# Expert weights split in larger pieces, and result additions issued one phase later

## The chip, the cores and the metric

The kernel runs on one core of one Trainium2 chip. The metric is device microseconds of one execution. Before the change it is 1491.45 us, the median of 3 runs (1490.14 to 1492.38). The profiled execution took 1492.99 us, of which 1490.9 us lie between its first and last instruction, at a mean granted TensorE clock of 0.988 of full speed.

## The reference, cut to what matters

Two decoder layers on 256 tokens of 1024 features. The second layer ends in a mixture of eight experts, and that part is all that the change touches:

```python
def swiglu(x, w_gate, w_up, w_down):
    return (jax.nn.silu(x @ w_gate) * (x @ w_up)) @ w_down

def moe_ffn(x, router_w, w_gate, w_up, w_down):      # top 2 of 8 experts for each token
    ...
    def expert_block(args):
        tok_b, e_b = args
        xb = xf[tok_b]                                # the expert's tokens
        return swiglu(xb, w_gate[e_b], w_up[e_b], w_down[e_b])
    ...                                               # w_gate, w_up: 8 x 1024 x 3584, w_down: 8 x 3584 x 1024
    y = y * w_buf[:, None]                            # times the gate
    out = jax.ops.segment_sum(y, tok_buf, num_segments=T)
```

All arrays are float32. The expert weights are 352 MB, read once.

## The kernel before, in words

**Splitting.** TensorE multiplies float32r. To keep float32 accuracy a weight piece `raw` is split in two: `wh`, the rounded copy, made by ScalarE (ACT, line 177), and `wl = raw - wh`, made by VectorE (DVE, line 180). The activations are split in the same way. TensorE (PE) then sums products: for a stationary block of activations it takes `wh` with the high and the low part and `wl` with the high part only.

**Pieces.** A piece is one load: 1 x 1792 columns of `w_gate` or `w_up` (896 KB), or 2 x 1024 of `w_down` (1 MB), into one of seven 8 KB buffers per partition ("ring"). `halves` splits it in two halves of 896 or 1024 columns, one instruction each on ACT and on DVE; the halves take turns between two pools, each with four pairs of 4 KB buffers (`wpool`, `wpool2`). A load into a ring buffer waits until DVE has split what was in it.

**Phases.** An expert's 3584 hidden features are done in two chunks of 1792 (`c` = 0, 1). Each chunk is a gate phase (8 pieces, PSUM banks "mm" and "gd"), then Silu into `hh` (line 1194), an up phase (8 pieces, the same bank names), the product into `hh` (line 1217), and later, woven into the next chunk's phases, its 7 down pieces, which add up in two banks "b". Four experts after the first are done in full width (128 tokens, "wide"), three in 64 tokens ("narrow": experts 2, 4 and 6 in order of time). A narrow expert stacks high and low activations in one stationary block, so each half needs 4 products for a wide one's 6. The last of its 8 pieces is not split; it is multiplied as float32, and the low rows are moved up through `room` (line 1121, ACT) and a product with `shift`. Silu, `room` and the multiplication into `hh` are pinned to their place in the order of their engine.

**Side work.** Lists of small steps (`side`) are popped one per piece: `to_features` (PE transposes `hh`, ACT and DVE make `hT`, lines 1137 to 1140), `combine` (two steps: ACT and DVE copy a result bank "b" into the one buffer `ys`, PE multiplies it with `DT` into a bank "a", DVE adds it to `x_in`, lines 1092 to 1099), `transposed` (makes `DT`), and `dispatch` (8 steps: PE gathers the next two experts' tokens with `D` into a bank "a", ACT copies them to `xg`, line 1023). In a second chunk the gate phase has 4 (narrow: 2) steps of `to_features`, 2 of `combine` and 1 of `transposed`; the up phase has the 8 of `dispatch`, when a group of experts is due. Bank "a" has two buffers. Each engine runs its instructions in one order, which a scheduler has fixed when the program was built, from the program's order and its own estimates; it can pull a step ahead of where the program has it.

Of the kernel before, what the change touches and what calls it, by code (L numbers as in the profile page):

```python
# [17 lines left out]
P = 128  # L18
T = 256
NB = 2  # L20
# [45 lines left out]
def trunk(ctx, tc, x, positions, w_in, conv_w, a_log, dt_bias, gdn_norm_w, lam_q1, lam_k1, lam_q2, lam_k2,  # L66
# [95 lines left out]
    def halves(ld, cut=1, count=2):  # L162

        raw, nk, cols = ld
        m = nk * cols // count
        for i in range(count):
            pool, size = wpool, WH
            if extra:
                turn[0] += 1
                if turn[0] % 2 == 0:  # L170
                    pool, size = extra[1], 1024
            wh = pool.tile([P, size], F32R, tag="wh", name=nm("wh"))
            wl = pool.tile([P, size], F32R, tag="wl", name=nm("wl"))
            n = m // (cut if i else 1)
            for c in range(0, m, n):
                w = raw[:, i * m + c:i * m + c + n]
                high = S.activation(wh[:, c:c + n], w, AF.Copy)  # L177
                if fence_high[0] is not None:
                    order(high, fence_high[0])
                low = V.tensor_tensor(wl[:, c:c + n], w, wh[:, c:c + n].bitcast(F32), op=ALU.subtract)  # L180
                if fence[0] is not None:
                    order(low, fence[0])
            yield i * (nk // count), wh, wl

    def piece(src, nk, cols, parts=1, cut=1):
        return halves(load(src, nk, cols, parts, cut), cut)
# [793 lines left out]
    def experts(xs, jobs, mp, ring2, rest, first):  # L980
# [22 lines left out]
        def dispatch(group, early=False):  # L1003
# [3 lines left out]
            Dt = mp.tile([P, NB, W], F32R, tag="ys", name=nm("D"))  # L1007
# [25 lines left out]
        def transposed(n):  # L1033
            Dt = mp.tile([P, NB, P], F32R, tag="ys", name=nm("D"))
# [16 lines left out]
        def products(outs, xg, narrow, k, parts, x32=None):  # L1051
# [5 lines left out]
            for i, (_, wh, wl) in enumerate(parts):  # L1057
                o = outs[2 * i:2 * i + 2]
                if not narrow:
                    xstat(o, [xg[:, 0:4], xg[:, 4:8]], k, 1, 0, wh, wl, CHUNK // 2, KD)  # L1060
                    continue
                x_ = xg[:, k].rearrange("p c s -> p (c s)")
                for w in (wh, wl):
                    for j in range(2):
                        mm(o[j], x_, w[:, j * BANK:(j + 1) * BANK], k == 0 and w is wh, False)

        def down_pieces(n, c, first=0, parts=1, cut=1):

            wd = weights(n, 2)[c * CHUNK:(c + 1) * CHUNK].rearrange("(p j) d -> p j d", j=NF)
            for f in range(first, NF, 2):  # L1070
                yield [(f + j, wh, wl) for j, wh, wl in piece(wd[:, f:f + 2, :], 2, D, parts, cut if f == NF - 2 else 1)]

        def down(subs, n, c, hT, py):
            for f, wh, wl in subs:
                K, k = NC * NF, c * NF + f
                if jobs[n][3]:
                    x_ = hT[:, f].rearrange("p c s -> p (c s)")
                    for w in (wh, wl):
                        for i, o in enumerate(py):
                            mm(o, x_, w[:, i * 512:(i + 1) * 512], k == 0 and w is wh, k == K - 1 and w is wl)  # L1080
                else:
                    for w in (wh, wl):
                        for c_ in range(2 if w is wh else 1):
                            for i, o in enumerate(py):
                                mm(o, hT[:, f, c_], w[:, i * 512:(i + 1) * 512], k == 0 and w is wh and c_ == 0,
                                   k == K - 1 and w is wl)

        def combine(n, py, DT):
            def part(i):
                ys = mp.tile([P, 2, 512], F32R, tag="ys", name=nm("ys"))  # L1090
                yh, yl = ys[:, 0], ys[:, 1]
                S.activation(yh, py[i], AF.Copy)  # L1092
                V.tensor_tensor(yl, py[i], yh.bitcast(F32), op=ALU.subtract)
                for b in range(NB):
                    pt = bank("a")
                    mm(pt, DT[:, b], yh, True, False)
                    mm(pt, DT[:, b], yl, False, True)
# [3 lines left out]
            return [lambda i=i: part(i) for i in range(2)]  # L1101
# [47 lines left out]
        side = []  # L1149
        tiles, steps = dispatch([jobs[n] for n in groups[0]], True)  # L1150
# [6 lines left out]
        for n, job in enumerate(jobs):  # L1157
# [5 lines left out]
            for c in range(NC):  # L1163
# [263 lines left out]
    with tc.tile_pool(name="ring2", bufs=1, reuse_waits="tile") as ring2, \  # L1427
            tc.tile_pool(name="wpool2", bufs=4, reuse_waits="tile") as wpool2, \
# [30 lines left out]
```

## Time and profile before

| | us |
|---|---|
| median of 3 runs | 1491.45 |
| profiled execution | 1492.99 |
| its span | 1490.9 |
| experts (from the first expert weights at work to the end) | some 540 to 1491 |
| PE busy | 1448.6 |
| DVE busy | 1218.3 |
| ACT busy | 1036.6 |

An engine's row says how long at least one of its instructions ran. For PE this includes the drain of pipelined matmuls, so it is not a measure of peak. The experts repeat: one wide and one narrow expert together take some 231 us, and the pattern returns with the next pair.

### The profile page before, as it was taken

To read this page: it belongs to the slowest core of one execution; us is meant where nothing else is said; L and a number is where in the kernel's file an instruction comes from. 1 tells how busy PE (TensorE), PEld (TensorE's weight loads), DVE (VectorE), ACT (ScalarE), POOL (GpSimd) and SP (SyncE) were. 2 spreads that over 40 slices of the span, in tenths; PEclk is the share of its full clock that TensorE was granted. 3 is DMA by queue.
4 is the path that set the end of the run, shared out by engine and by line. 5 is a ranking of instruction groups with operands and counts; after the bars stand their busy time and mean duration, and the time that the engine had idled before them with its cause. 6 is when DMAs were issued, how large, how long until landed. Compare 5 with 4: busy or idle time off the path is not lost.

```text
span 1490.9 us, 24038 instructions
## 1 busy us (share of the span) xinstructions
PE 1448.6 (97%) x8873; PEld 1233.1 (83%) x8873; DVE 1218.3 (82%) x1609; ACT 1036.6 (70%) x1553; POOL 23.7 (2%) x37
## 2 busy tenths in 40 slices
PE   8999999999999999999999999999999999999995
PEld 8978899998987889886698877588877589888884
DVE  6877655556796798989899989899989899989886
ACT  5748544456666587787797887886887877778763
POOL 1100000000000000000000000000000000000000
PEclk9999999999999999999999999999999999999998
DMA  9633455535533179999999999999999899999891
GB/s 322 219 106 118 153 195 195 193 121 196 193 113 100 54 298 363 386 371 374 380 394 384 375 390 394 356 393 408 352 379 417 335 395 413 338 357 395 292 394 34
DMA packets 89124, 433.93 MB, mean 291 GB/s; under 512 B 7816, under 2 KB 9992, under 8 KB 74912
## 3 DMA queue, kind: packets, MB, share of 16 engines
q1 hardware_dynamic: 87808, 428.54, 76.1%
q0 software_dynamic: 1184, 3.71, 0.9%
q8 instruction: 73, 1.20, 0.3%
q14 instruction: 59, 0.48, 0.1%
HBM read 431.17 MB, written 1.05 MB: 290 GB/s over the span
## 4 chain that ended last, share of the span: by engine, by line
PE 87%; DVE 7%; issue 2%; ACT 2%; DMA 0%; DVEq 0%; SPq 0%; ACTq 0%
PE ps_b L99 26%; PE ps_mm L99 25%; PE ps_gd L99 24%; PE ps_a L99 9%; DVE wl L180 4%; PE ps_a L1137 2%; ACT wh L177 1%; DVE x_in L1099 1%; PE ps_mm L566 0%; ACT junk L415 0%; DVE hT L1140 0%; ACT xT L240 0%; PE ps_gd L408 0%; PE ps_mm L670 0%; DVE D L999 0%
## 5 line engine op out<-in xcount | busy, mean ns | idle before, releaser
L180 DVE TENSOR_TENSOR wl<-raw,wh 128x896 fp32r<-128x896 f32 (+2 forms) x851 | 925.7, 1144 | 145.8 <-ACT wh L177 139.4
L177 ACT ACTIVATE wh<-raw 128x896 fp32r<-128x896 f32 (+2 forms) x851 | 792.4, 995 | 153.4 <-PE ps_gd L99 68.4
L99 PE MATMUL ps_b<-wh,hT 128*128 128x512 f32 x816 | 232.6, 396 | 0.7 <-ACT hT L1139 0.7
L99 PE MATMUL ps_gd<-wh,xg 128*128 128x448 f32 x808 | 218.8, 368 | 0.0
L99 PE MATMUL ps_mm<-wh,xg 128*128 128x448 f32 x808 | 212.5, 372 | 0.3
L99 PEld LDWEIGHTS ps_b<-wh,hT 128*128 128x128 f32 x816 | 152.0, 188 | 39.2 <-issue 6.4
L99 PEld LDWEIGHTS ps_gd<-wh,xg 128*128 128x128 f32 x808 | 151.9, 189 | 12.7
L99 PE MATMUL ps_b<-wl,hT 128*128 128x512 f32 x492 | 159.0, 400 | 2.2 <-DVE wl L180 2.2
L99 PEld LDWEIGHTS ps_mm<-wh,xg 128*128 128x128 f32 x808 | 147.6, 189 | 16.4 <-ACT wh L177 2.0
L99 PE MATMUL ps_gd<-wl,xg 128*128 128x448 f32 x488 | 142.9, 374 | 8.9 <-DVE wl L180 7.2
L99 PE MATMUL ps_mm<-wl,xg 128*128 128x448 f32 x488 | 140.7, 369 | 0.1
L99 PEld LDWEIGHTS ps_b<-wl,hT 128*128 128x128 f32 x492 | 90.9, 188 | 31.9 <-DVE wl L180 6.7
L99 PEld LDWEIGHTS ps_gd<-wl,xg 128*128 128x128 f32 x488 | 88.8, 188 | 27.7 <-DVE wl L180 20.2
L99 PEld LDWEIGHTS ps_mm<-wl,xg 128*128 128x128 f32 x488 | 90.9, 188 | 11.7 <-DVE wl L180 4.3
L1139 ACT ACTIVATE hT<-ps_a 128x512 fp32r<-128x512 f32 (+2 forms) x52 | 27.4, 544 | 64.8 <-PE ps_a L1137 37.7
L99 PE MATMUL ps_mm<-xT,wh 128*128 128x256 f32 x448 | 70.9, 280 | 0.0
L99 PEld LDWEIGHTS ps_mm<-xT,wh 128*128 128x128 f32 x448 | 60.8, 189 | 0.4
L1140 DVE TENSOR_TENSOR hT<-ps_a,hT 128x512 fp32r<-128x512 f32 (+2 forms) x52 | 31.8, 621 | 26.5 <-ACT hT L1139 26.5
L99 PE MATMUL ps_gd<-xT,wh 128*128 128x256 f32 x320 | 50.5, 280 | 0.0
L1092 ACT ACTIVATE ys<-ps_b 128x512 fp32r<-128x512 f32 x14 | 8.4, 599 | 53.2 <-PE ps_b L99 39.0
L99 PE MATMUL ps_mm<-xT,wl 128*128 128x256 f32 x224 | 44.6, 280 | 0.0
L99 PEld LDWEIGHTS ps_gd<-xT,wh 128*128 128x128 f32 x320 | 43.1, 189 | 0.0
(407 smaller groups left out, 1660.2 us busy)
## 6 DMA issues: line engine op xcount, KB each, us to landing
raw<-in_moe_w_gate_dram SPq DMA_DIRECT2D x128, 896.0 KB, 8.2
raw<-in_moe_w_up_dram SPq DMA_DIRECT2D x128, 896.0 KB, 6.6
raw<-in_moe_w_down_dram SPq DMA_DIRECT2D x110, 1024.0 KB, 8.1
raw<-in_w_in_dram SPq DMA_DIRECT2D x24, 1024.0 KB, 6.6
raw<-in_ffn_w_gate_dram SPq DMA_DIRECT2D x11, 1024.0 KB, 5.1
raw<-in_ffn_w_up_dram SPq DMA_DIRECT2D x11, 1024.0 KB, 5.1
raw<-in_ffn_w_down_dram SPq DMA_DIRECT2D x11, 1024.0 KB, 4.9
raw<-in_w_out_dram SPq DMA_DIRECT2D x8, 1024.0 KB, 4.9
```

What stands on the lines that cost most here:

```text
L99: return PE.matmul(o, lhsT, rhs, start=start, stop=stop, skip_group_check=True)
L177: high = S.activation(wh[:, c:c + n], w, AF.Copy)
L180: low = V.tensor_tensor(wl[:, c:c + n], w, wh[:, c:c + n].bitcast(F32), op=ALU.subtract)
L1092: S.activation(yh, py[i], AF.Copy)
L1099: V.scalar_tensor_tensor(o, pt, jobs[n][2][:, b], o, op0=ALU.mult, op1=ALU.add)
L1137: PE.transpose(pt[:, f * w:(f + 1) * w], hv[:, f0 + f], ident[rows, rows])
L1139: S.activation(hT[:, f0:f0 + n_, 0], pv, AF.Copy)
L1140: V.tensor_tensor(hT[:, f0:f0 + n_, 1], pv, hT[:, f0:f0 + n_, 0].bitcast(F32), op=ALU.subtract)
```

## The change

Of the pieces of `w_gate`, `w_up` and `w_down` that come through `piece` uncut, every second one (a counter, `turn`) is split by one instruction on ACT and one on DVE, over its whole 1792 or 2048 columns, into a buffer of 8 KB from `wpool2`, which now has two pairs of 8 KB instead of four of 4 KB. The others are split in halves as before, all four halves from `wpool`. Products with a whole piece take all four banks for one stationary block, first all of `wh`, then all of `wl`; for a down piece `wh` of both rows comes ahead of `wl`. `combine` gives two lists: the two copies (with two `ys` buffers) stay in the gate phase; the two additions, and `transposed`, are carried on to the list of the up phase, in front of `dispatch`, whose preparation becomes a step of its own.

```diff
+    class Whole(list):
+        pass
-    def halves(ld, cut=1, count=2):
+    def halves(ld, cut=1, count=2, parts=1):
         raw, nk, cols = ld
+        if extra and cut == 1 and parts == 1:
+            turn[0] += 1
+            if turn[0] % 2 == 0:
+                n = nk * cols
+                wh = extra[1].tile([P, WC], F32R, tag="wh", name=nm("wh"))
+                wl = extra[1].tile([P, WC], F32R, tag="wl", name=nm("wl"))
+                high = S.activation(wh[:, :n], raw[:, :n], AF.Copy)
...
+                low = V.tensor_tensor(wl[:, :n], raw[:, :n], wh[:, :n].bitcast(F32), op=ALU.subtract)
...
+                return Whole((k, wh[:, k * cols:(k + 1) * cols], wl[:, k * cols:(k + 1) * cols]) for k in range(nk))
+        return split(ld, cut, count)
+
+    def split(ld, cut, count):
...
-            pool, size = wpool, WH
-            if extra:
-                turn[0] += 1
-                if turn[0] % 2 == 0:
-                    pool, size = extra[1], 1024
-            wh = pool.tile([P, size], F32R, tag="wh", name=nm("wh"))
-            wl = pool.tile([P, size], F32R, tag="wl", name=nm("wl"))
+            wh = wpool.tile([P, WH], F32R, tag="wh", name=nm("wh"))
+            wl = wpool.tile([P, WH], F32R, tag="wl", name=nm("wl"))
@@ products
-                o = outs[2 * i:2 * i + 2]
+                m = 4 if isinstance(parts, Whole) else 2
+                o = outs[m * i:m * i + m]
@@ down
-            for f, wh, wl in subs:
+            turns = [(sub[0], i, sub[i]) for sub in subs for i in (1, 2)]
+            if isinstance(subs, Whole):
+                turns.sort(key=lambda t: t[1])
+            for f, part, w in turns:
@@ combine
-            def part(i):
-                ys = mp.tile([P, 2, 512], F32R, tag="ys", name=nm("ys"))
+            def copy(i):
+                ys = mp.tile([P, 2, 512], F32R, tag="ys", name=nm("ys"), bufs=2)
...
+            def add(i):
                 for b in range(NB):
                     pt = bank("a")
...
-            return [lambda i=i: part(i) for i in range(2)]
+            return [lambda i=i: copy(i) for i in range(2)], [lambda i=i: add(i) for i in range(2)]
@@ experts, between the gate and the up phase
+                side, carry = carry, []
                 if c == NC - 1 and groups and n + 1 not in xgs:
-                    group = groups.pop(0)
-                    tiles, side = dispatch([jobs[g] for g in group])
-                    xgs.update(zip(group, tiles))
+                    def gather(group=groups.pop(0), side=side):
+                        tiles, steps = dispatch([jobs[g] for g in group])
+                        xgs.update(zip(group, tiles))
+                        side.extend(steps)
+                    side.append(gather)
@@ experts, after the up phase
                 if pend and pend[1] == NC - 1:
-                    side += combine(pend[0], pend[3], DT)
+                    copies, carry = combine(pend[0], pend[3], DT)
+                    side += copies
                 if c == 0:
...
-                    side.append(lambda n=n, later=later: later.append(transposed(n)))
+                    carry.append(lambda n=n, later=later: later.append(transposed(n)))
@@ pools
-            tc.tile_pool(name="wpool2", bufs=4, reuse_waits="tile") as wpool2, \
+            tc.tile_pool(name="wpool2", bufs=2, reuse_waits="tile") as wpool2, \
```

Where this moves instructions, three places. The first is ACT at the end of the gate phase of a narrow expert's second chunk (`room` and `hh` as above, each `wh` a split). Before:

```order
L1121 ACTIVATE room_9598<-ps_gd_9410 64x448
L177 ACTIVATE wh_9624<-raw_9622 128x1024
L177 ACTIVATE wh_9628<-raw_9622 128x1024
L177 ACTIVATE wh_9646<-raw_9644 128x1024
L1194 ACTIVATE hh_9607<-ps_mm_9407 64x448
L1194 ACTIVATE hh_9607<-ps_mm_9408 64x448
L1194 ACTIVATE hh_9607<-ps_gd_9409 64x448
L1194 ACTIVATE hh_9607<-ps_gd_9410 64x448
L177 ACTIVATE wh_9650<-raw_9644 128x1024
```

and with the change:

```order
L1147 ACTIVATE room_9267<-ps_gd_9118 64x448
L195 ACTIVATE wh_9293<-raw_9291 128x1024
L195 ACTIVATE wh_9297<-raw_9291 128x1024
L177 ACTIVATE wh_9315<-raw_9313 128x2048
L1221 ACTIVATE hh_9276<-ps_mm_9115 64x448
L1221 ACTIVATE hh_9276<-ps_mm_9116 64x448
L1221 ACTIVATE hh_9276<-ps_gd_9117 64x448
L1221 ACTIVATE hh_9276<-ps_gd_9118 64x448
L195 ACTIVATE wh_9333<-raw_9331 128x896
```

Ahead of the four pinned Silu instructions stood three halves; now two halves and a whole piece stand there, four halves' worth.

The second is PE at the end of the up phase of a wide expert's second chunk, where the tokens of the next pair are gathered (`D` times `xs`, into a bank "a"). Before, one step of four products after each weight piece:

```order
L99 MATMUL ps_gd_8583<-wl_8777,xg_6452 128x448
L99 MATMUL ps_gd_8584<-wl_8777,xg_6452 128x448
L99 MATMUL ps_a_8786<-D_8585,xs_5509 128x192
L99 MATMUL ps_a_8786<-D_8585,xs_5510 128x192
L99 MATMUL ps_a_8786<-D_8585,xs_5509 128x192
L99 MATMUL ps_a_8786<-D_8585,xs_5510 128x192
L99 MATMUL ps_mm_8581<-wh_8795,xg_6452 128x448
L99 MATMUL ps_mm_8582<-wh_8795,xg_6452 128x448
L99 MATMUL ps_mm_8581<-wh_8795,xg_6452 128x448
L99 MATMUL ps_mm_8582<-wh_8795,xg_6452 128x448
```

and with the change, the third, fourth and part of the fifth of five such steps in a row:

```order
L99 MATMUL ps_a_8561<-D_8441,xs_5509 128x192
L99 MATMUL ps_a_8561<-D_8441,xs_5510 128x192
L99 MATMUL ps_a_8561<-D_8441,xs_5509 128x192
L99 MATMUL ps_a_8561<-D_8441,xs_5510 128x192
L99 MATMUL ps_a_8568<-D_8441,xs_5509 128x192
L99 MATMUL ps_a_8568<-D_8441,xs_5510 128x192
L99 MATMUL ps_a_8568<-D_8441,xs_5509 128x192
L99 MATMUL ps_a_8568<-D_8441,xs_5510 128x192
L99 MATMUL ps_b_8266<-wh_8584,hT_8068 128x512
L99 MATMUL ps_a_8575<-D_8441,xs_5509 128x192
L99 MATMUL ps_a_8575<-D_8441,xs_5510 128x192
L99 MATMUL ps_a_8575<-D_8441,xs_5509 128x192
```

Between these five steps only one product of a weight piece is left (`ps_b`).

The third is ACT at that same place, which copies the gathered tokens of each step to the two experts' `xg`. Before:

```order
L177 ACTIVATE wh_8708<-raw_8706 128x896
L177 ACTIVATE wh_8718<-raw_8706 128x896
L1023 ACTIVATE xg_8588<-ps_a_8670 128x128
L1023 ACTIVATE xg_8589<-ps_a_8670 128x256
L177 ACTIVATE wh_8737<-raw_8735 128x896
L177 ACTIVATE wh_8747<-raw_8735 128x896
L177 ACTIVATE wh_8766<-raw_8764 128x896
```

and with the change:

```order
L1041 ACTIVATE xg_8444<-ps_a_8547 128x128
L1041 ACTIVATE xg_8445<-ps_a_8547 128x256
L1041 ACTIVATE xg_8444<-ps_a_8554 128x128
L1041 ACTIVATE xg_8445<-ps_a_8554 128x256
L177 ACTIVATE wh_8628<-raw_8626 128x2048
L1041 ACTIVATE xg_8444<-ps_a_8561 128x128
L1041 ACTIVATE xg_8445<-ps_a_8561 128x256
L1041 ACTIVATE xg_8444<-ps_a_8568 128x128
L1041 ACTIVATE xg_8445<-ps_a_8568 128x256
L195 ACTIVATE wh_8646<-raw_8644 128x1024
L195 ACTIVATE wh_8650<-raw_8644 128x1024
L1041 ACTIVATE xg_8444<-ps_a_8575 128x128
```

The copies of two steps now stand together, and a split of 2048 columns lies between those of the second and the third of the five steps.

## Rows read from the trace of the kernel before

**Rows 1.** page, part 1: busy us (share of the span) xinstructions, by engine
```profile
PE 1448.6 (97%) x8873; PEld 1233.1 (83%) x8873; DVE 1218.3 (82%) x1609; ACT 1036.6 (70%) x1553; POOL 23.7 (2%) x37
```

**Rows 2.** busy time by stretch; engine busy us (xinstructions), PEclk, DMA share
```profile
core 0: us, PE busy (x) PEld busy (x) DVE busy (x) ACT busy (x) POOL busy (x), PEclk, DMA share, GB/s
882.30:906.90 24.60, 24.60 (x107) 18.69 (x105) 21.31 (x21) 22.92 (x30) 0.00 (x0) 1.00 1.01 404
906.90:940.50 33.60, 31.57 (x135) 22.83 (x135) 30.39 (x36) 21.11 (x28) 0.00 (x0) 1.00 0.95 362
940.50:965.10 24.60, 23.73 (x93) 15.62 (x92) 21.02 (x20) 23.16 (x31) 0.00 (x0) 1.00 0.90 364
992.70:1018.40 25.70, 25.70 (x124) 23.01 (x123) 25.46 (x26) 23.89 (x29) 0.00 (x0) 1.00 1.02 419
```

**Rows 3.** the chain that ended last, experts, 540 to 1491 us, by line
```profile
by line: PE ps_b L99 29.1%; PE ps_mm L99 26.4%; PE ps_gd L99 26.1%; DVE wl L180 6.0%; issue 2.8%; PE ps_a L1137 2.7%; PE ps_a L99 2.3%; DVE x_in L1099 0.9%; ACT wh L177 0.5%; DVE hT L1140 0.4%; DVE o L1281 0.3%; DVE D L999 0.2%; DVE o L1276
```

**Rows 4.** waits, 540 to 1490 us: who for whom, us, times, longest
```profile
DVE wl L180 <- ACT wh L177: 42.8, 50, 3.2
ACT xg L1023 <- PE ps_a L99: 24.9, 18, 5.1
PEld ps_gd L99 <- DVE wl L180: 20.2, 31, 1.6
ACT ys L1092 <- PE ps_a L99: 14.2, 7, 3.8
DVE ys L1093 <- ACT ys L1092: 6.5, 4, 4.6
ACT wh L177 <- DMA raw<-in_moe_w_down_dram: 4.5, 9, 0.6
```

**Rows 5.** the DMA queue's own waits, same stretch
```profile
SPq L157 <- DVE wl L180: 653.5, 326, 7.5
```

**Rows 6.** costliest groups by form, 540 to 1490 us: busy, mean ns, idle before
```profile
L180 DVE TENSOR_TENSOR wl<-raw,wh 128x896 fp32r<-128x896 f32 x476 | 487.6, 1086 | 21.5 <-ACT wh L177 19.2
L177 ACT ACTIVATE wh<-raw 128x896 fp32r<-128x896 f32 x472 | 413.6, 951 | 16.9 <-PE ps_b L99 6.6 <-PE ps_gd L99 4.1 <-PE ps_mm L99 4.0
L180 DVE TENSOR_TENSOR wl<-raw,wh 128x1024 fp32r<-128x1024 f32 x223 | 259.7, 1220 | 23.7 <-ACT wh L177 23.6
L177 ACT ACTIVATE wh<-raw 128x1024 fp32r<-128x1024 f32 x223 | 222.1, 1055 | 10.4 <-DMA raw<-in_moe_w_down_dram 4.5 <-PE ps_mm L99 3.0 <-PE ps_gd L99 1.6
```

**Rows 7.** order of time, DVE, 876 to 912 us: start, us, merged instructions
```profile
878.05 4.63 DVE L180 TENSOR_TENSOR wl<-raw,wh 128x1024 fp32r<-128x1024 f32 x4 [0.75 <-ACT wh L177]
884.95 16.39 DVE L180 TENSOR_TENSOR wl<-raw,wh 128x896 fp32r<-128x896 f32 x16 [2.27 <-ACT wh L177]
902.36 4.63 DVE L180 TENSOR_TENSOR wl<-raw,wh 128x1024 fp32r<-128x1024 f32 x4 [1.02 <-ACT wh L177]
```

**Rows 8.** the same of ACT, 884 to 912 us
```profile
883.97 13.78 ACT L177 ACTIVATE wh<-raw 128x896 fp32r<-128x896 f32 x16
```

**Rows 9.** the same of DVE, 936 to 966 us
```profile
943.31 17.52 DVE L180 TENSOR_TENSOR wl<-raw,wh 128x1024 fp32r<-128x1024 f32 x17 [3.22 <-ACT wh L177]
```

**Rows 10.** the same of ACT, 931 to 966 us
```profile
935.50 2.95 ACT L177 ACTIVATE wh<-raw 128x1024 fp32r<-128x1024 f32 x3
940.51 0.96 ACT L1194 ACTIVATE hh<-ps_mm 64x448 f32<-64x448 f32 x2 [2.06 <-PE ps_mm L99]
```

**Rows 11.** the chain, 1049 to 1082 us, by line
```profile
by line: PE ps_mm L99 30.1%; PE ps_gd L99 29.9%; PE ps_b L99 23.5%; PE ps_a L99 10.0%; DVE wl L180 6.5%; DVE D L999 1.0%; issue 0.1%
```

**Rows 12.** order of time, weight loads on PE, 1049 to 1066 us
```profile
1061.12 0.62 PEld L99 LDWEIGHTS ps_a<-D,xs 128*128 128x128 f32 x4
1061.66 0.71 PEld L99 LDWEIGHTS ps_mm<-wh,xg 128*128 128x128 f32 x4
```

**Rows 13.** the same of ACT, 1036 to 1070 us
```profile
1043.79 0.60 ACT L1092 ACTIVATE ys<-ps_b 128x512 fp32r<-128x512 f32 x1 [3.78 <-PE ps_a L99]
1061.95 0.55 ACT L1023 ACTIVATE xg<-ps_a 128x128 fp32r<-128x128 f32 x2 [4.27 <-PE ps_a L99]
```

More of the change, by code (lines that the diff above doesn't have):

```diff
@@ L160, in load @@
         return raw, nk, cols
-    def halves(ld, cut=1, count=2):
+    class Whole(list):
+        pass
+    def halves(ld, cut=1, count=2, parts=1):
+        raw, nk, cols = ld
+        m = nk * cols // count
+        if extra and cut == 1 and parts == 1:
[5 more added lines that the diff above has]
+                high = S.activation(wh[:, :n], raw[:, :n], AF.Copy)
+                if fence_high[0] is not None:
+                    order(high, fence_high[0])
+                low = V.tensor_tensor(wl[:, :n], raw[:, :n], wh[:, :n].bitcast(F32), op=ALU.subtract)
+                if fence[0] is not None:
+                    order(low, fence[0])
+                return Whole((k, wh[:, k * cols:(k + 1) * cols], wl[:, k * cols:(k + 1) * cols]) for k in range(nk))
+        return split(ld, cut, count)
+    def split(ld, cut, count):
         raw, nk, cols = ld
@@ L185, in piece @@
     def piece(src, nk, cols, parts=1, cut=1):
-        return halves(load(src, nk, cols, parts, cut), cut)
+        return halves(load(src, nk, cols, parts, cut), cut, parts=parts)
     pre_ctx = ExitStack()
@@ L1006, in dispatch @@
             W = sum(ws)
-            Dt = mp.tile([P, NB, W], F32R, tag="ys", name=nm("D"))
+            Dt = mp.tile([P, NB, W], F32R, tag="ys", name=nm("D"), bufs=2)
             for j, job in enumerate(group):
@@ L1033, in transposed @@
         def transposed(n):
-            Dt = mp.tile([P, NB, P], F32R, tag="ys", name=nm("D"))
+            Dt = mp.tile([P, NB, P], F32R, tag="ys", name=nm("D"), bufs=2)
             slots(Dt, jobs[n], True)
@@ L1063, in products @@
                 for w in (wh, wl):
-                    for j in range(2):
+                    for j in range(m):
                         mm(o[j], x_, w[:, j * BANK:(j + 1) * BANK], k == 0 and w is wh, False)
@@ L1070, in down_pieces @@
             for f in range(first, NF, 2):
-                yield [(f + j, wh, wl) for j, wh, wl in piece(wd[:, f:f + 2, :], 2, D, parts, cut if f == NF - 2 else 1)]
+                subs = piece(wd[:, f:f + 2, :], 2, D, parts, cut if f == NF - 2 else 1)
+                yield (Whole if isinstance(subs, Whole) else list)((f + j, wh, wl) for j, wh, wl in subs)
         def down(subs, n, c, hT, py):
-            for f, wh, wl in subs:
+            turns = [(sub[0], i, sub[i]) for sub in subs for i in (1, 2)]
@@ L1075, in down @@
+            if isinstance(subs, Whole):
+                turns.sort(key=lambda t: t[1])
+            for f, part, w in turns:
                 K, k = NC * NF, c * NF + f
+                last = k == K - 1 and part == 2
                 if jobs[n][3]:
                     x_ = hT[:, f].rearrange("p c s -> p (c s)")
-                    for w in (wh, wl):
+                    for i, o in enumerate(py):
+                        mm(o, x_, w[:, i * 512:(i + 1) * 512], k == 0 and part == 1, last)
+                else:
+                    for c_ in range(2 if part == 1 else 1):
@@ L1079, in down @@
                         for i, o in enumerate(py):
[L1080 to L1086, printed above, removed]
@@ L1088, in combine @@
-        def combine(n, py, DT):
-            def part(i):
-                ys = mp.tile([P, 2, 512], F32R, tag="ys", name=nm("ys"))
-                yh, yl = ys[:, 0], ys[:, 1]
-                S.activation(yh, py[i], AF.Copy)
-                V.tensor_tensor(yl, py[i], yh.bitcast(F32), op=ALU.subtract)
+                            mm(o, hT[:, f, c_], w[:, i * 512:(i + 1) * 512], k == 0 and part == 1 and c_ == 0, last)
+        def combine(n, py, DT):
+            parts = []
+            def copy(i):
+                ys = mp.tile([P, 2, 512], F32R, tag="ys", name=nm("ys"), bufs=2)
+                S.activation(ys[:, 0], py[i], AF.Copy)
+                V.tensor_tensor(ys[:, 1], py[i], ys[:, 0].bitcast(F32), op=ALU.subtract)
+                parts.append(ys)
+            def add(i):
@@ L1094, in part @@
                 for b in range(NB):
                     pt = bank("a")
-                    mm(pt, DT[:, b], yh, True, False)
-                    mm(pt, DT[:, b], yl, False, True)
+                    mm(pt, DT[:, b], parts[i][:, 0], True, False)
+                    mm(pt, DT[:, b], parts[i][:, 1], False, True)
                     o = x_tok[:, b, i * 512:(i + 1) * 512]
                     V.scalar_tensor_tensor(o, pt, jobs[n][2][:, b], o, op0=ALU.mult, op1=ALU.add)
-            return [lambda i=i: part(i) for i in range(2)]
+            return [lambda i=i: copy(i) for i in range(2)], [lambda i=i: add(i) for i in range(2)]
@@ L1149, in experts @@
         side = []
+        carry = []
         tiles, steps = dispatch([jobs[n] for n in groups[0]], True)
```

2 lines of the change are left out of this document (1 added, 1 removed).

## The prediction

> **What bounds the kernel now.** I read the page first, then the expert part by stretches, the chain that ended last, the waits, and last the order of time on DVE and ACT where DVE stands still. The page shows PE busy for 97% of the span and DVE for 82% [rows 1], but PE's figure includes draining, so the stretches decide. They follow one narrow expert from its first up phase, and one phase of the wide expert after it: PE 24.60 of 24.60 us, 31.57 of 33.60, 23.73 of 24.60, then 25.70 of 25.70; DVE 21.31, 30.39, 21.02 and 25.46 in the same stretches [rows 2]. So PE is the limit in the wide expert and in a narrow one's first chunk, with DVE close behind, and in a narrow one's second chunk PE has gaps. The chain agrees: its three largest entries are weight products on PE with 81.6% together, and the DVE split has 6.0% of the 951 us, 57 us [rows 3]. The waits say which instruction PE lacked: `wl`, for 20.2 us in 31 waits ahead of products into "gd" alone, while DVE lacked `wh` from ACT for 42.8 us in 50 waits [rows 4]. The loads are not it, though the DMA share is 0.90 to 1.02 [rows 2]: the DMA queue stands for 653.5 us because DVE has not yet freed a buffer [rows 5], and ACT waits on the main kind of late load, down weights, for 4.5 us only [rows 4]. The bound is thus PE, and in narrow second chunks DVE, which starves when ACT is held at an instruction that waits for PE.
>
> **The change, part by part.** The built program has 176 whole pieces among the experts, so 176 instructions fewer on ACT and on DVE. Products, loads and the moment at which a piece's `raw` is free (the end of its last `wl`) stay as they were.
>
> (a) Fewer calls. A DVE split takes 1086 ns for 896 columns and 1220 for 1024 [rows 6]: 1.047 ns a column and 148 ns fixed. But a run of 16 (14 of 896, 2 of 1024, in the order of the program) took 16.39 us [rows 7], where the single durations add up to 17.64; so neighbours overlap by 1.25/15 = 83 ns, and a call that goes gives back 65 ns. On ACT the fixed part is 1055 - 128 x 8 x (1055 - 951)/128 = 223 ns [rows 6], the same run took 13.78 us [rows 8] for 15.42, an overlap of 109 ns, so 114 ns a call. For DVE that is 176 x 0.065 = 11.4 us. It counts only where DVE is last. Ends: 0, if PE hides all of it, and -11.4. I take half, -5.7: DVE and PE alternate as the later one. The Trainium skill (Perfetto Trace Analysis, Optimizing Scalar/DVE Operations) puts the overhead of an SBUF instruction at about 60 ns on DVE and says that the profiled latency is about twice the busy share, because the second half overlaps with the next instruction. This trace agrees, with 65 of 148 ns; the 148 taken for itself would make 26 us of the 11.4.
>
> (b) Two `ys` buffers, both copies in a row. Before, the second copy waited for the products of the first: ACT stood 14.2 us in 7 waits, and DVE behind it 6.5 us in 4 [rows 4]; the longest in the pattern, 3.78 us at 1043.79 [rows 13], lies in a phase of a wide expert. The additions themselves do not shrink, and the scheduler keeps PE's part of them around the end of the gate phase, so moving them is nothing by itself. Ends 0 and -6.5; I take -1, since most of the DVE waits are in one place.
>
> (c) One half more ahead of Silu in the narrow second chunk. Before, ACT did 3 halves from 935.50 on, then waited 2.06 us for PE to bring the rows together [rows 10]; DVE ran out and stood 3.22 us until 943.31 [rows 9]. With the change 4 halves' worth lie there, so DVE has 1.22 us less the overlap, 1.14 us, more to do in that gap. Three such chunks: -3.4. Ends 0 (if the fourth half is not needed any sooner) and 3 x 3.22 = -9.7.
>
> (d) A whole piece first after a held ACT. DVE can start only when ACT has done all of its columns. At three restarts of a narrow expert's first chunk, where DVE stood 0.75, 2.27 and 1.02 us [rows 7], the program now has a whole piece first: 2048, 1792 and 2048 columns. On ACT, 2048 take 223 + 2048 x 0.8125 = 1887 ns for 1055, and 1792 take 1679 for 951 [rows 6]. That is 0.83 + 0.73 + 0.83 = 2.39 us of DVE time an expert, 7.2 for three. In the stretch with the third of these restarts PE was still busy all 24.60 us [rows 2], so DVE's idle time there was covered by the lead it has over PE. It costs only as far as the lead is missed in the second chunk: a third, +2.4; ends 0 and +7.2. Behind the late DVE stand PE and, through the ring, the loads.
>
> (e) Gathering in one go. With the two additions, `transposed` and the preparation in front, five of the eight steps now come after the last up piece, back to back, with two banks "a". A step of four products takes PE 0.54 us (1061.12 to 1061.66 [rows 12]); ACT starts the copies 0.3 us after a step is done and takes 0.55 us a pair [rows 13]. So step 3 waits for the copies of step 1, some 0.4 us, and step 5 for those of step 3, which stand behind a split of 2048 columns (1.89 us): counted through, step 3 ends at 2.0 us, its copies at 4.2, and PE, with one weight product in hand, stands from 2.7 to 4.2. Together 1.9 us, in four places (three pairs and the last single expert, taken alike): 7.6. Queued behind on PE are the down pieces; behind them Silu's successors on ACT. In that phase the chain is PE for 93.5% [rows 11], so PE's loss counts; against it stands that ACT's waits ahead of these copies, 24.9 us in 18 [rows 4], one of them 4.27 us [rows 13], come later and partly go, and that a narrow expert follows, in which PE catches up with DVE anyway. I take half, +3.8; ends 0 and +7.6. The same skill page (Optimizing Tensor Performance, Matmuls) wants independent matmul groups to rotate through different banks so that copying one out overlaps the next group; before, a weight piece lay between two steps and did this with two banks [rows 12]; the rows show no step without it. By that rule the full 7.6 would count and the sum would be near nothing.
>
> The order of the down products (`wh` of both rows first) I cost at nothing: PE takes the same number, and DVE's lead hides that `wl` comes later. Without the lead, a phase's end has four products left after the last `wl` rather than two, about half of the 0.71 us that four loads take [rows 12], 0.36 us at two ends of three chunks, 2.1 us.
>
> Sum: -5.7 - 1.0 - 3.4 + 2.4 + 3.8 = -3.9 us. Against the profiled execution, 1492.99 us (span 1490.9 and 2.1 around it), that is 1489.1; the median of the runs lies 1.5 below that execution, so I predict 1487.5 us.
>
> **The rivals.** A: DVE is last throughout. Then (a) counts in full and so does (d), and PE's pause in (e) is covered: -11.4 - 1.0 - 3.4 + 7.2 = -8.6, 1482.9 us. For it: 25.46 of 25.70 us of DVE in a wide phase. Against: PE has no gap in that phase [rows 2].
>
> B, slower: PE is last throughout, and the gathering decides. Relief on DVE and ACT is then worth nothing, and PE's four pauses count in full: +7.6, 1499.1 us. For it: the chain of that phase [rows 11]. Against: the 57 us of DVE in the whole chain [rows 3]. It decides if ACT does the 2048 columns ahead of the third step's copies while PE has nothing but these steps left.
>
> C: neither gets through. PE is busy nearly all the time, a narrow second chunk is tied to PE at `room`, Silu and the features' copies, and what DVE gains it waits for at the next of these: 1491.5 us. For it: PE's 24.60 and 25.70 us without a gap; against, the gaps in the second chunk [rows 2].
>
> D, slower: the coarse pieces cost more than their calls save. DVE is not full in a narrow expert (21.31 of 24.60 us, 21.02 of 24.60 [rows 2]) and starves at restarts, so (a) is lost and (d) counts in full with the 2.1 us at phase ends: +9.3, 1500.8 us. Against it: DVE's starving did not reach PE in the first chunk. The skill's section on Scalar/DVE operations says as much: engines that are not saturated but cause bubbles on others may do better with instructions broken up, and this trace, with 42.8 us of DVE waiting for `wh` [rows 4], has some of that.
>
> **How the numbers follow.** Forecast 0.42, with its own range from 1483 to 1491.5; A 0.16; B 0.15; C 0.16; D 0.11. The low end of the range is A with two thirds of what (c) could still give, 1482.9 - 4.2, about 1478.5; the high end takes in B and D, 1501. I give 1478 to 1501. A measurement of this kernel tells 0.2%, 3 us, from no change. The forecast's case is beyond that in about two thirds: 0.28; with A and a little of C, faster is 0.46. Same: 0.11 of the forecast's and 0.13 of C, 0.24. Slower: B, D and the rest, 0.30.
>
> **What would show it.** Right: the mean of a 1792-column split near 2.02 us on DVE and 1.68 on ACT; DVE's gap ahead of 943 us shorter by about 1 us in all three narrow experts; the gaps of the first chunk's restarts longer by 0.7 to 0.8; ACT's wait of `ys` for bank "a" gone; a stop of 1.5 us on PE's loads of `D` products at four places; the DVE split's share of the chain below 6.0%. Wrong: larger pieces that cost more or less than their columns; a PE gap in wide phases other than at the gathering; ACT held for the two big buffers, which I cost at nothing because PE is through with a whole piece two pieces before the next one needs its place.

## The result, and the profile after

The changed kernel took 1501.14 us, the median of 6 runs (1497.0 to 1506.06), against 1490.63 for the kernel before in the same session: a ratio of 1.0076, 95% interval 1.0059 to 1.0093. The forecast was 1487.5. The profiled execution took 1500.64 us, its span is 1498.5, its mean granted clock 0.989. A ratio's 0.001 is 1.49 us; below, differences are given so, because each session has its own runs of the kernel before. One run further down, of 1589.76 us at a mean granted clock of 0.845 (the change with both stops mended), is left out of that kernel's median and ratio.

First the page, busy us by engine, beside [rows 1]:

```profile
PE 1444.5 (96%) x8873; PEld 1231.3 (82%) x8873; DVE 1205.2 (80%) x1433; ACT 1021.9 (68%) x1377; POOL 23.8 (2%) x37
```

and the chain of the expert part, 540 to 1498 us, by line, beside [rows 3]:

```profile
by line: PE ps_b L99 25.6%; PE ps_mm L99 25.2%; PE ps_gd L99 24.0%; issue 4.4%; DVE wl L180 4.2%; DVE wl L198 3.0%; ACT wh L177 2.8%; PE ps_a L1163 2.7%; PE ps_a L99 1.8%; ACT wh L195 1.2%; ACT hh L1221 0.9%; DVE x_in L1125 0.8%; ACT xg L10
```

The 176 calls are gone, and with them 13.1 us of DVE's work and 14.7 of ACT's. PE, whose work is unchanged, is busy for a smaller share of a longer span, and ACT has come into the chain (`wh` had 0.5% [rows 3], now 2.8 and 1.2). DVE's splits have 4.2 and 3.0, together 7.2%, where the prediction's sign of being right was less than 6.0. The waits, 540 to 1498 us, in total, times, longest (line 180 and 177 are whole pieces now, 198 and 195 halves), beside [rows 4]:

```profile
DVE wl L180 <- ACT wh L177: 62.9, 54, 4.0
ACT wh L177 <- PE ps_gd L99: 27.9, 32, 1.2
ACT xg L1041 <- PE ps_a L99: 26.5, 9, 7.3
PEld ps_mm L99 <- DVE wl L180: 18.6, 27, 1.2
DVE wl L198 <- ACT wh L195: 12.9, 17, 2.8
PEld ps_b L99 <- DVE wl L180: 5.6, 4, 1.4
PEld ps_a L99 <- ACT xg L1041: 4.7, 6, 1.6
PEld ps_a L1057 <- DVE D L1017: 4.0, 3, 1.3
PEld ps_mm L99 <- ACT hh L1221: 3.2, 1, 3.2
```

DVE's wait for `wh` went from 42.8 us to 62.9 + 12.9: more than the work it was spared came back as waiting. On PE the waits for `wl` ahead of "gd" have turned into waits ahead of "mm", the first product of a piece: with one operation for the piece, nothing of its `wl` is ready before all of it is. Three waits of PE are new: 4.7 us for `xg`, 4.0 for `D`, and 3.2 for `hh`, the first Silu.

The stretches that answer to [rows 2], moved with the phases:

```profile
887.60:912.60 25.00, 24.58 (x106) 18.39 (x105) 19.76 (x16) 22.23 (x24) 0.00 (x0) 1.00 0.99 383
912.60:946.00 33.40, 31.46 (x137) 23.02 (x136) 31.40 (x32) 21.57 (x24) 0.00 (x0) 1.00 0.95 362
946.00:970.80 24.80, 23.66 (x100) 16.86 (x98) 22.38 (x17) 23.06 (x26) 0.00 (x0) 1.00 1.01 406
997.20:1023.60 26.40, 26.40 (x128) 23.64 (x127) 25.67 (x19) 23.50 (x23) 0.00 (x0) 1.00 0.99 407
```

In these steady phases little moved: 25.0 us for 24.6, 33.4 for 33.6, 24.8 for 24.6. The fourth, an up phase of the wide expert, took 26.4 us for 25.7, but the gate phase ahead of it 26.4 (970.80 to 997.20) for 27.6. In the first, DVE is busy for 19.76 us where it was for 21.31, and the phase is no shorter. So the loss is at particular places, and three could be read.

**The first Silu.** Weight loads on PE, then ACT, both in order of time (start, us, merged instructions, in brackets the idle time before):

```profile
545.07 0.39 PEld L99 LDWEIGHTS ps_gd<-wl,xg 128*128 128x128 f32 x2
548.66 0.50 PEld L99 LDWEIGHTS ps_mm<-wh,xg 128*128 128x128 f32 x2 [3.21 <-ACT hh L1221]
```

```profile
545.06 1.70 ACT L177 ACTIVATE wh<-raw 128x1792 fp32r<-128x1792 f32 x1 [1.09 <-PE ps_gd L99]
546.77 1.28 ACT L1221 ACT_TABLE_LOAD   x1
548.07 0.98 ACT L1221 ACTIVATE hh<-ps_mm 128x448 f32<-128x448 f32 x2
```

In the first chunk there are no down products to do while Silu empties the gate banks. The last gate piece ends all four banks together; ACT is held until 545.06 for one of the two big buffers, which PE's last products use, then splits 1792 columns, loads Silu's table and begins. PE stands 3.21 us. Before the change the same place read, ACT and then PE's loads:

```profile
545.36 0.95 ACT L177 ACTIVATE wh<-raw 128x896 fp32r<-128x896 f32 x1 [0.27 <-PE ps_gd L99]
546.34 1.28 ACT L1194 ACT_TABLE_LOAD   x1
```

```profile
548.23 0.30 PEld L99 LDWEIGHTS ps_mm<-wh,xg 128*128 128x128 f32 x2 [0.41 <-ACT hh L1194]
```

**The gathering.** PE's loads and ACT at the end of the second up phase of the expert before 1090 us:

```profile
1084.87 1.06 PEld L99 LDWEIGHTS ps_a<-D,xs 128*128 128x128 f32 x8
1086.30 0.97 PEld L99 LDWEIGHTS ps_a<-D,xs 128*128 128x128 f32 x8 [0.37 <-ACT xg L1041]
1087.19 0.19 PEld L99 LDWEIGHTS ps_b<-wh,hT 128*128 128x128 f32 x1
1088.98 0.52 PEld L99 LDWEIGHTS ps_a<-D,xs 128*128 128x128 f32 x4 [1.60 <-ACT xg L1041]
```

```profile
1085.69 1.00 ACT L1041 ACTIVATE xg<-ps_a 128x128 fp32r<-128x128 f32 x4 [0.29 <-PE ps_a L99]
1086.58 1.91 ACT L177 ACTIVATE wh<-raw 128x2048 fp32r<-128x2048 f32 x1
1088.38 1.00 ACT L1041 ACTIVATE xg<-ps_a 128x128 fp32r<-128x128 f32 x4
```

Five steps in a row, a 2048-column split between the copies, stops of 0.37 and 1.60 us, as worked out. They stand in full at two of the four places (855.68 us has 1.61 too); the first has 0.48, the last 0.25.

**The transposed weights.** In each narrow second gate phase PE now waits 1.3 us for `D`, which DVE makes behind the two additions (the row of 4.0 us above).

### The profile page after: what moved, and what is told of

Its sections match the earlier page's. It is cut to its first block, busy times and chain, and to the rows that moved or that the text cites. A ratio compares the mean times of both kernels' runs of the same rounds, so it can differ in the third digit from the quotient of the medians.

```text
span 1498.5 us, 23519 instructions
## 1 busy us (share of the span) xinstructions
PE 1444.5 (96%) x8873; PEld 1231.3 (82%) x8873; DVE 1205.2 (80%) x1433; ACT 1021.9 (68%) x1377; POOL 23.8 (2%) x37
## 4 chain that ended last, share of the span: by engine, by line
PE 83%; DVE 7%; ACT 6%; issue 4%; DMA 0%; DVEq 0%; ACTq 0%; SPq 0%
PE ps_mm L99 24%; PE ps_b L99 23%; PE ps_gd L99 23%; PE ps_a L99 9%; DVE wl L180 3%; DVE wl L198 3%; ACT wh L177 2%; PE ps_a L1163 2%; ACT wh L195 2%; ACT hh L1221 1%; DVE x_in L1125 1%; PE ps_mm L584 0%; ACT xg L1041 0%; ACT junk L433 0%; ACT xT L258 0%
## 5 line engine op out<-in xcount | busy, mean ns | idle before, releaser
L198 DVE TENSOR_TENSOR wl<-raw,wh 128x896 fp32r<-128x896 f32 (+2 forms) x499 | 560.0, 1152 | 112.2 <-ACT wh L195 107.8
L195 ACT ACTIVATE wh<-raw 128x896 fp32r<-128x896 f32 (+2 forms) x499 | 485.2, 1003 | 141.8 <-PE ps_gd L99 66.5
L180 DVE TENSOR_TENSOR wl<-raw,wh 128x1792 fp32r<-128x1792 f32 (+1 forms) x176 | 369.9, 2102 | 62.9 <-ACT wh L177 62.9
L177 ACT ACTIVATE wh<-raw 128x1792 fp32r<-128x1792 f32 (+1 forms) x176 | 311.2, 1768 | 43.3 <-PE ps_gd L99 29.0
L99 PE MATMUL ps_mm<-wh,xg 128*128 128x448 f32 x808 | 223.4, 372 | 3.6 <-ACT hh L1221 2.8
L99 PE MATMUL ps_b<-wh,hT 128*128 128x512 f32 x816 | 225.9, 397 | 0.7 <-ACT hT L1165 0.7
L99 PE MATMUL ps_b<-wl,hT 128*128 128x512 f32 x492 | 147.7, 396 | 3.9 <-DVE wl L180 3.9
L99 PE MATMUL ps_gd<-wl,xg 128*128 128x448 f32 x488 | 139.6, 367 | 0.0
L1165 ACT ACTIVATE hT<-ps_a 128x512 fp32r<-128x512 f32 (+2 forms) x52 | 27.6, 542 | 82.1 <-PE ps_a L1163 55.8
```

Source lines behind the costliest of these rows:

```text
L99: return PE.matmul(o, lhsT, rhs, start=start, stop=stop, skip_group_check=True)
L177: high = S.activation(wh[:, :n], raw[:, :n], AF.Copy)
L180: low = V.tensor_tensor(wl[:, :n], raw[:, :n], wh[:, :n].bitcast(F32), op=ALU.subtract)
L1165: S.activation(hT[:, f0:f0 + n_, 0], pv, AF.Copy)
```

## The experiments

Each was run in five rounds beside the kernel before. Medians, ratio to the kernel before with its interval:

| kernel | us | ratio |
|---|---|---|
| the change | 1501.14 | 1.0076 (1.0059 to 1.0093) |
| whole pieces alone | 1497.1 | 1.0048 (1.0031 to 1.0065) |
| carried additions alone | 1496.41 | 1.0044 (1.0029 to 1.0059) |
| change, two steps a piece | 1498.83 | 1.0044 (1.0027 to 1.0061) |
| change, last gate piece in halves | 1498.89 | 1.0052 (1.0033 to 1.0071) |
| change, both | 1495.01 | 1.0030 (1.0015 to 1.0046) |
| whole pieces in wide experts | 1493.84 | 1.0023 (1.0009 to 1.0036) |
| big buffers, by halves | 1490.85 | 1.0005 (0.9991 to 1.0020) |
| carried additions, two steps a piece | 1497.02 | 1.0039 (1.0023 to 1.0056) |
| whole pieces, first chunk by halves | 1492.57 | 1.0006 (0.9992 to 1.0020) |
| carried, two steps, transposed back | 1495.09 | 1.0024 (1.0007 to 1.0042) |
| two `ys` buffers alone | 1488.5 | 0.9978 (0.9962 to 0.9994) |
| change, all three edits | 1491.17 | 0.9990 (0.9976 to 1.0003) |

**One half of the change at a time.** Whole pieces with `combine`, `transposed` and `dispatch` as before; and the side work of the change with all pieces in halves.

```diff
 # whole pieces alone
-                    copies, carry = combine(pend[0], pend[3], DT)
-                    side += copies
+                    side += combine(pend[0], pend[3], DT)
 # carried additions alone
+                side, carry = carry, []
```

> The whole pieces alone; copies, additions, transposed and gathering stand as before the change. Theory 1 (PE pauses at two places: in the gathering of five steps in a row, about 1.9 us at each of four, and once at the first chunk's Silu, about 3 us; the larger splits are worth nothing net): only the Silu pause stays, so 1493 to 1495 us against some 1490.6 before. Theory 2 (the coarse pieces themselves cost, by late restarts of DVE and by their two big buffers): nearly the whole loss stays, 1498 to 1501.

> The result additions and transposed one phase later, with the second buffer and the gathering behind them, but all pieces in halves as before the change. Theory 1: the four gathering pauses stay and the Silu pause goes, 1496 to 1499 us (shorter if no split of 2048 columns stands between the copies: a half of 1024 takes 0.83 us less, so 1494 to 1497). Theory 2: no loss, 1489 to 1492.

Both halves are slower, by 7.2 and 6.6 us. The second is where theory 1 had it; the first lies between the two theories, so neither accounts for it alone.

**The two stops, one at a time and together.** Two list steps after each of the first four up pieces where a gathering is due, so that no steps pile up behind the last; and the first chunk's last gate piece in halves.

```diff
-                    if side:
-                        side.pop(0)()
+                    for _ in range(2 if due and sub[0] < 4 else 1):
+                        if side:
+                            side.pop(0)()
 # the other
-            if turn[0] % 2 == 0:
+            if turn[0] % 2 == 0 and not apart[0]:
```

> The changed kernel, but where a gathering is due two steps of the list are done after each of the first four up pieces, so that no five gathering steps stand in a row; at most two do. Theory 1: the gathering pauses of PE go, 7 us less than the changed kernel, 1492 to 1495 us. Theory 2: no change from it, 1499 to 1502.

> The changed kernel, but the last gate piece of the first chunk is split in halves, so that two of the four banks are done a half piece earlier and their Silu lies beside PE's work on the other two. Theory 1: PE's pause of 3.2 us at 548 us shrinks to about 0.4, and the halved clock behind it may go too: 2.5 to 4 us less than the changed kernel, about 1497.5 us. Theory 2: within 1 us of the changed kernel.

> The changed kernel with both earlier edits: two list steps behind each of the first four up pieces where a gathering is due, and the last gate piece of the first chunk in halves. Theory 1 (the loss is the products' stop at the four gatherings, 1.97 us each, and at the first Silu, about 2.3 us): 1501.1 - 7.9 - 2.3 = 1491, so 1490 to 1493. Theory 2 (most of it is the larger pieces themselves, in the narrow experts): the two edits take off what each took off alone, 2.3 + 2.2, so 1496 to 1498.

With two steps a piece, a weight piece stands between two gathering steps and PE does not stop:

```profile
1080.80 0.62 PEld L99 LDWEIGHTS ps_a<-D,xs 128*128 128x128 f32 x4
1081.34 0.71 PEld L99 LDWEIGHTS ps_mm<-wh,xg 128*128 128x128 f32 x4
```

The ratio fell by only 0.0032 (4.8 us) and 0.0024 (3.6), with intervals that overlap the change's, and both together came to 1.0030. Theory 1 needed 1490 to 1493 and failed; some 4.5 us were still to be found.

**Size of the operation or of the buffer; wide or narrow.** Big buffers filled by two operations of half the columns; and whole pieces in wide experts only, with that filling in the narrow ones and the first chunk's last piece apart.

```diff
+            if big:
+                wh, wl = wh2[:, i * m:(i + 1) * m], wl2[:, i * m:(i + 1) * m]
```

> Buffers as in the change (two pairs of 2048 columns for four of 1024), but each is filled by two operations of half the columns; the list of side work as before the change. If the size of the operation costs (it ends late for the product that waits for its first half): as the kernel before, 1490 to 1492. If the buffers cost (they come free only in pairs, so the copies into them are held): as the kernel with whole pieces alone, 1496 to 1498. The saved fixed time of 176 operations is given up, so up to 5.7 us more may be seen if DVE sets the pace: to 1502.

> One operation per piece in the wide experts alone; in the narrow ones the same 2048-column buffers are filled by two operations, one for each half; the last gate piece of the first chunk in halves; the list of side work as before the change. Theory 1 (larger operations cost nothing but the first Silu): as the kernel with whole pieces alone less about 2 us, 1494 to 1496. Theory 2 (the larger operations cost 2.2 us in each narrow expert pair and save 1.0 us in each wide expert, as the phases of the kernel with whole pieces alone show): 1491 - 4 = 1487, so 1485 to 1489.

The buffers cost nothing: 1.0005, though ACT waits for them 23.3 us in 23. So the price of whole pieces is the operation's size, or the order of the products that comes with it: this kernel also multiplies by halves again, and no run separates the two. Whole pieces in wide experts alone came to 1.0023, at 1493.84 us just below theory 1's 1494 and far from theory 2's 1485 to 1489: without whole pieces in the narrow experts, and with the last gate piece apart, half of the loss remained, and the saving that the phases of wide experts had seemed to show did not come.

**The start.** Whole pieces alone, but the first expert's first chunk filled by halves.

```diff
-            if turn[0] % 2 == 0:
+            if turn[0] % 2 == 0:
+                if starting[0]:
+                    return split(ld, cut, count, True)
...
+                starting[0] = False        # after the first chunk
```

> Whole pieces alone, but in the first expert's first chunk the big buffers are filled by two operations of half the columns. Theory 1 (a larger operation costs where the products run up with nothing split ahead: the first gate phase was 2.6 us longer and its up phase 1.3 us): 1497.1 - 3.5 = 1493.6, so 1492 to 1495. Theory 2 (it costs at every late piece of the narrow experts, 1.3 us in a pair of experts, and the start is a part of the launch's scatter): 1496 to 1498.

From 1.0048 to 1.0006, as theory 1 had it: 6.3 us (3 to 9.5 by the two intervals), nearly all that whole pieces cost, lay in the first 40 us of the expert part. With the halves there PE's stop at the first Silu is short again:

```profile
544.64 0.30 PEld L99 LDWEIGHTS ps_mm<-wh,xg 128*128 128x128 f32 x2 [0.52 <-ACT hh L1224]
```

The rows explain some 3 us of stop at Silu, and 0.9 more where the first up phase ends (a gap of 1.1 us between two weight loads, which the kernels in halves don't have). The other 2 us are not put down to a place, and are within the interval.

**Where the carried additions cost.** Two steps a piece without whole pieces; then with `transposed` back in the gate's list ahead of the copies.

```diff
+                own = len(side)            # behind the steps of to_features
...
-                    carry.append(lambda n=n, later=later: later.append(transposed(n)))
+                    side.insert(own, lambda n=n, later=later: later.append(transposed(n)))
```

> The kernel before with the result additions behind up alone (halves as before), and two list steps behind each of the first four up pieces where a gathering is due. Theory 1 (moving the additions costs only what the gathering in a row makes the products stop): 1496.4 - 4 x 1.5 = 1490.4, so 1489 to 1492. Theory 2 (the additions behind up cost by themselves, where they stand between the up products): as without the second step, 1495 to 1497.

> The kernel with the additions carried and two list steps behind an up piece, with the transposed weights' step back in the gate phase's list, ahead of the two copies. Theory 1 (behind the additions its D comes late, the products stop 1.35 us for it and 1.62 us for the next split right behind, and the granted clock falls in some executions): 1490 to 1492.5, with a mean granted clock of 0.990 to 0.992 instead of 0.988. Theory 2 (the additions cost by themselves, among the up products): 1495 to 1498, clock as before the edit.

Theory 1 failed both times: 1.0039, then 1.0024, and these differ by less than their intervals. The mean granted clock of the last stayed at 0.988 (12 runs; the kernel before had 0.9905 in 35 runs of that session), as theory 2 had it, though its cause, the additions among the up products, was not tested. The trace shows what the edit missed. The wait for `D` is gone, but the wait for the next `wl` behind it took its time over: instead of several shorter stops, one of 2.28 us, in the load after the last gate products.

```profile
932.47 0.42 PEld L99 LDWEIGHTS ps_b<-wh,hT 128*128 128x128 f32 x2
935.18 0.19 PEld L99 LDWEIGHTS ps_b<-wl,hT 128*128 128x128 f32 x1 [2.28 <-DVE wl L180]
936.41 0.23 PEld L99 LDWEIGHTS ps_mm<-raw,xg 128*64 128x64 f32 x1 [0.52 <-ACT wh L177]
```

And here are the stretches of 3 us around it (busy us of each engine, then the granted clock):

```profile
933.00:936.00 3.00, 1.15 (x4) 0.47 (x3) 3.00 (x4) 2.93 (x3) 0.00 (x0) 0.94 0.77 287
936.00:939.00 3.00, 3.00 (x5) 0.92 (x4) 3.00 (x4) 0.00 (x0) 0.00 (x0) 0.50 0.58 151
```

PE was busy 1.15 of 3 us; in the next 3 the clock granted was 0.50, 1.2 GHz for 2.4, and the phase came out 2.0 us longer than before. The trace has this stop of 2.28 us in all three narrow second gate phases: after the third the clock fell to 0.50 as well (1168 to 1171 us), after the first it stayed at 1.00 (702 to 708 us). The kernel without the `transposed` edit has the same after its 1.36 and 1.62 us stops at 937 us (0.55 in 939 to 942). Before the change PE lacked as much there in total, but in stops of 0.48, 0.46, 1.62, 0.41 and 1.04 us with products between, and the clock stayed at 1.00 [rows 2].

**The second buffer alone, and all mended.** The kernel before with two `ys` buffers; and the change with all three edits (two steps, `transposed` back, first chunk by halves).

```diff
-                ys = mp.tile([P, 2, 512], F32R, tag="ys", name=nm("ys"))
+                ys = mp.tile([P, 2, 512], F32R, tag="ys", name=nm("ys"), bufs=2)
...                                        # the same for D, which shares these buffers, in two places
```

> The kernel before with two ys buffers and nothing else. If the second copy's wait (ACT 14.2 us in 7 waits) is worth what the prediction took: 1490.5 - 1.0 = 1489.5, so 1489 to 1490.3, down to 1484 if DVE's 6.5 us behind it counted in full. If the products hide it: 1490 to 1492, the same.

> The changed kernel with all three edits: two list steps behind each of the first four up pieces where a gathering is due, the transposed weights' step back in the gate phase's list, and the first expert's first chunk by halves in the big buffers. If the losses add up (gathering some 3 us, transposed some 2, start some 3.5): 1501.1 - 8.5 = 1492.6, so 1491.5 to 1494. If the larger pieces in the narrow experts cost by themselves: 1495 to 1497. Below 1489 would mean that the saved operations pay once these three are mended.

Two buffers alone are 0.9978 (0.9962 to 0.9994): 3.3 us faster than the kernel before, and the lowest median of all. `D` shares the buffers and has two as well, here and in the change; which of them gives the gain is not separated. ACT's wait of 3.78 us for bank "a" [rows 13] is gone, and it runs its splits there without a stop until it waits for Silu's banks:

```profile
1035.40 8.13 ACT L177 ACTIVATE wh<-raw 128x896 fp32r<-128x896 f32 x9
1047.07 0.98 ACT L1194 ACTIVATE hh<-ps_mm 128x448 f32<-128x448 f32 x2 [3.53 <-PE ps_mm L99]
```

Every second gate phase from the second expert on became 0.5 to 0.6 us shorter; the wide experts' up phases behind them gave some 0.4 back, and 2.4 us stayed. All three edits take the change from 1.0076 to 0.9990, that is 12.8 us: the whole loss goes with them. It is a little better than the sum expected (1491.5 to 1494), but the saved operations don't pay beyond the second buffer.

The parts do not simply add. The kernel in halves with the same two edits of the list has 1.0024, so there the whole pieces, with the first chunk by halves, took off 0.0034 or 5.1 us, while with the side work as before they were worth nothing (1.0006). The longest stop in the narrow second gate phases is 1.49 us here, for 2.28 there; the clock of this trace is 1.00 from 546 to 1479 us, and its mean in 12 runs is 0.9912, for 0.9882. Whether the shorter stops are the reason was not tested.

```profile
931.06 0.30 PEld L99 LDWEIGHTS ps_mm<-wl,xg 128*128 128x128 f32 x2 [1.49 <-DVE wl L183]
```

## Why the prediction was wrong, step by step

Two steps failed most. The first chunk of the expert part got no term, and measured +6.3 us; moving the additions was taken as nothing by itself, and together with the gathering, for which 3.8 was put down, it measured +9.9.

**(a) and (c), with (d): wrong in what they were worth.** The sizes of the operations were right: 1792 columns take 2018 ns on DVE for 2.02 us, and 1703 on ACT for 1.68. But the three terms, -6.7 us together, measured +0.9 (whole pieces with the first chunk by halves, interval -1.2 to +3.0). Half of (a) was taken to count because "DVE and PE alternate as the later one". In that kernel's trace PE's weight loads do wait less for `wl` between 560 and 1470 us, 28.0 us for 31.2, but all their waits together are 79.1 us for 77.6: what `wl` gave came back ahead of other instructions, most of it at `room`, 7.2 us for 4.4. That is rival C's mechanism. (c) had the right sign at its place, and more: the gap ahead of Silu's successors is 2.06 us shorter than [rows 9], where 1 us was worked out.

```profile
948.73 2.09 DVE L198 TENSOR_TENSOR wl<-raw,wh 128x896 fp32r<-128x896 f32 x2 [1.16 <-ACT wh L195]
```

The phase that holds it, 33.4 us for 33.6, shows what that is worth. (d)'s restarts are longer at two of the three places, 0.75 to 2.10 and 1.02 to 2.09 us, and not at the third, 2.27 to 2.15:

```profile
884.36 2.29 DVE L180 TENSOR_TENSOR wl<-raw,wh 128x2048 fp32r<-128x2048 f32 x1 [2.10 <-ACT wh L177]
891.07 2.03 DVE L180 TENSOR_TENSOR wl<-raw,wh 128x1792 fp32r<-128x1792 f32 x1 [2.15 <-ACT wh L177]
909.28 2.29 DVE L180 TENSOR_TENSOR wl<-raw,wh 128x2048 fp32r<-128x2048 f32 x1 [2.09 <-ACT wh L177]
```

The rule of the Trainium skill that rival D named (Perfetto Trace Analysis, Optimizing Scalar/DVE Operations: an engine that is not saturated but leaves others waiting may do better with instructions broken up) is what the first chunk shows, with 6.3 us for breaking up its whole pieces again: ACT, idle for 1.09 us just before, there kept PE standing 3.21 us.

**No term for the start: the largest thing left out.** The working followed the repeating pattern and treated the first chunk as one more of it. It is the one chunk without down products, where nothing covers PE while Silu waits behind ACT's larger split: +6.3 us, of which rows show some 3.7. The last line of "wrong" named part of the cause, ACT held for the two big buffers, and costed it at nothing; ACT was held 27.9 us in 32 waits, and this mattered in that one place. The kernel with big buffers filled by halves shows that the holding alone is free.

**(b): right, too small.** -1.0 was taken of 0 to -6.5; the second buffer alone is worth -3.3. The upper end was misread: DVE's 6.5 us behind ACT [rows 4] are still 6.5 us in 4 waits with two buffers, so only ACT's wait hung on the buffer.

**"Moving them is nothing by itself": wrong.** Carried additions with two buffers cost 6.6 us, 9.9 more (6.6 to 13.1 by the two intervals) than two buffers without the carrying. (e) put 3.8 on this, from stops of 1.9 us at four places counted half. The stops were 1.97 us where they came in full and 4.7 us in all, so that term was near; by edits it is worth 0.7 us with halves and 4.8 with whole pieces, where the splits between ACT's copies are the long ones. What was left out is that the additions and `transposed`, moved behind other work, bunch PE's stops at the end of a narrow second gate phase. In the trace of the carried additions in halves, PE's loads wait for `D` and `xg`, and with two buffers alone for neither:

```profile
PEld ps_a L1039 <- DVE D L999: 4.1, 3, 1.4
PEld ps_a L99 <- ACT xg L1023: 4.0, 7, 0.9
```

From the first Silu to the end, that trace takes 946.0 us and the one of two buffers alone 940.6, with the clock at 1.00 in both up to their last 13 us. So some 5.4 of the 9.9 us are there without a lower clock. The clock may be the rest: the mean granted clock of the three kernels with carried additions in halves was 0.9890, 0.9881 and 0.9882 in 11, 10 and 12 runs, against 0.9911, 0.9913 and 0.9905 for the kernel before in their sessions; over 1490 us that is an estimated 3 to 5 us. Lower clocks behind the bunched stops are seen in two of the three traces, not in that of the additions alone. So this part stays open.

By the terms: start +6.3, whole pieces otherwise +0.9, second buffer -3.3, carrying +9.9, 13.8 in all for 11.3 measured. The sum is 2.5 us too high, about half the width of one interval; the kernel with all three edits shows that the parts act on each other.

**The rivals.** The time lies 0.14 us above the range and just above B (1499.1: relief on DVE and ACT worth nothing, the gathering in full) and D (1500.8: coarse pieces cost more than they save). It was some of both at once: by edits, the gathering is worth 4.8 of B's 7.6 us, and the coarse pieces 7.2 of D's 9.3, though nearly all at the start and not at D's restarts. They had 0.26 together. C is what the whole pieces show once the start is mended, 1.0006.

## What to carry to other kernels

A pattern's cost is worked out in the steady state, but a coarser operation is paid for where nothing is in flight: look up the first round and each restart, and ask what covers PE there. A saved operation on an engine that is not last was worth nothing here by itself, and its waits have to be read again; a second buffer that takes away ACT's wait for PE was worth more than 176 saved calls. Moving work between phases should be checked for what it gathers into one long stop, not only for its own length.

## What the runs showed of the hardware

The times of one kernel scatter with the clock: of the kernel before, 33 runs in one session lie between 1484.84 us at a mean granted clock of 0.995 and 1494.21 at 0.989. Its profile in stretches of 3 us puts what it lost ahead of the expert part, at 0.50 to 0.64 near 9, 93, 105, 465, 513 and 528 us, and after 1479 us. In the changed kernel one more stands behind the first Silu's stop:

```profile
546.00:552.00 6.00, 3.33 (x10) 3.01 (x11) 3.17 (x4) 4.85 (x7) 0.00 (x0) 0.72 1.01 417
```

The same stop of 3.2 us in the kernel with whole pieces alone was followed by a clock of 1.00, so one and the same stop does not always bring it.
